# Mixer A's values as feature tiles turned by transposes, weight tiles fetched three ahead, bias tiles of several heads in one transfer

## The chip, the core and the metric

The kernel runs on one core of a Trainium2 chip. The metric is the device time of one execution in microseconds (us). The core's engines are TensorE (PE: matmuls, with PEld for its weight loads), VectorE (DVE), ScalarE (ACT), GpSimd (POOL) and SyncE (SP), which issues nearly all DMA transfers of this program from one queue, in order.

## The reference

One decoder layer for a prompt of 1024 tokens and 8 single-token samples, with shared weights:

```
h = RMSNorm(x)
qa, ka, va, za, qb, kb, vb, zb, qc, zc, ga, gb, gc = split(h @ w_in)
x + W_out( sum_i sigmoid(g_i) * P_i( mixer_i * silu(z_i) ) )
  mixer A: dilated causal attention, 8 heads x 64, patterns (window, stride) (128,1), (512,4), (2048,16),
           combined by their softmax denominators
  mixer B: sliding-window attention (128), 8 query heads, 2 kv heads x 64, with a learned sink per head
  mixer C: cross-attention, 4 heads x 128, into 256 memory tokens
  A and B add a relative-position bias (32 buckets); queries and keys are RMS-normed
```

Keys and values of A and B for prompt and samples, and of the memory, are outputs too. All is float32; the change concerns `va`, the 512 value columns of mixer A.

## The kernel before, in words

Every float32 product is made of three reduced-precision ones: each operand is split into a rounded part and a remainder (`hh` and `hl` of the normed input, `wh` and `wl` of a weight), and PE runs high x high, low x high, high x low. The prompt and the samples form one matrix of 1032 columns (tokens), kept as 8 feature tiles of 128 partitions and cut into three chunks of 344. A weight tile covers 128 output features (128 x 1024 numbers, 512 KB) and serves three units, one for each chunk; a unit is 24 matmuls (8 feature tiles x 3 products) into one PSUM bank `psD`, of which there are two. Then ACT evicts it.

A weight tile goes through three steps: a transfer into `wr` (`wfetch`, L289), a rounding into `wh` on ACT or POOL (`wlead`), and a subtraction into `wl` on DVE or POOL (`wrest`). Which tile is fetched when is set by `wpump`, `wnext` and `wget` (L307 to L338): `wahead(n, ...)` fetches all tiles below n; `wget` forces whatever is missing at the moment of use.

The order of all work is written by the program itself, as a recording. `main` yields after each half or whole unit; each yield is one `tick` (L241), which may put in a step of the attention pipeline (`rope`, with duos of two 128-blocks), a step of the sample work, deferred pieces (`when`), and a pump of weights. A class `Pace` keeps estimated engine times; `idle` (L236) says whether DVE and ACT lie less than 3 us behind PE in that estimate, and only then does the tick call `wpump`. Each engine then executes its own instructions strictly in the recorded order, waiting on semaphores; so does SP with its transfers.

Nearly all working tiles are slabs (128 x 1032 numbers), 47 buffers that are reused in turn (`SLABS`, L39): the first writer of a slab waits for the last readers of the tile that had it before. Small tiles have their own few buffers; the evicted values `c` have two.

After the memory's keys and values, the four query tiles of mixer C, and keys, values and queries of B comes `va_phase` (L744). Here the tokens lie on the partitions: for each half of the value columns (two weight tiles of `w_va`) and each block of 128 tokens (nine, the last with the 8 samples) 24 matmuls with 256 columns give psD; ACT evicts it into `c`; a transfer writes it to the output `o_va`; POOL rounds it and DVE subtracts, into a slab `vhl`; two transfers write that to the scratch arrays `vsc` (natural order) and `vsr` (stride order). `whold` holds back splits of further weights during the first five blocks. Then come queries and keys of A, the gates of z and g, the three branches and the output. Meanwhile the attention heads run, C first, then B, then A; A's heads read `vsc` and `vsr` with `v_load`, and fetch their bias (`bn`, `bias`) from the replicated table `rep` with `bias_tile`.

Of the kernel before, what the change touches and what calls it, by code (L numbers as in the profile page):

```python
# [30 lines left out]

AHEAD_FIRST, AHEAD = 3, 2
SPLIT_FIRST, SPLIT = 3, 2
# [137 lines left out]
class Kern:  # L171
# [153 lines left out]
    def wnext(self):  # L325

        i = self.wi
        if self.wr == i < self.wh and self.ok(self.wsp[i][0]):
            self.wahead(0, 0, i + 1)
        if not self.whold and self.wh == i < self.wd and self.ok(self.wraw[i]):  # L330
            self.wahead(0, i + 1, 0)

    def wpump(self):
        self.wahead(self.wi + self.wdepth, 0, 0)
        if self.wr < self.wh and (self.start and self.wr <= self.wi or self.ok(self.wsp[self.wr][0])):
            self.wahead(0, 0, self.wr + 1)
        if not self.whold and self.wh < min(self.wi + self.wsoon, self.wd) and self.ok(self.wraw[self.wh]):
            self.wahead(0, self.wh + 1, 0)  # L338
# [405 lines left out]
    def va_phase(self):  # L744
        nc, io = self.nc, self.io
        self.vsc, self.vsr = [self.dram([NP, 8, 2, 64], F32, "vhl") for _ in range(2)]

        def turn(half, v):
            p = self.psT()
            for t in range(2):  # L750
                nc.tensor.transpose(p[:, t * NS:(t + 1) * NS], v[:NS, t * P:(t + 1) * P], self.ident[:NS, :NS])
            nc.scalar.activation(self.vs_a[:, 2 * half:2 * half + 2], p[:, :2 * NS].rearrange("p (t b) -> p t b", t=2), AF.Copy)

        for half in range(2):
            cs = slice(half * 256, (half + 1) * 256)
            ws = [self.wget() for _ in range(2)]
            for tb in range(9):
                self.whold = tb < 5
                m = P if tb < 8 else NS
                d = self.ps("D", 2)  # L760
                s = slice(tb * P, tb * P + m)
                for j, (x, y, k) in enumerate(self.order(8)):
                    c = (k % 4) * 256
                    nc.tensor.matmul(d[:m, :256], self.h[k][y][:, s], ws[k // 4][x][:, c:c + 256], start=j == 0, stop=j == 23)
                v = self.small([P, CH], "c1", 2)[:, :256]
                nc.scalar.activation(v[:m], d[:m, :256], AF.Copy)
                nc.sync.dma_start(out=io["o_va"][tb * P:tb * P + m, cs], in_=v[:m])
                if tb < 8:
                    vhl = self.slab(F32R, "vhl")[:, :512]
                    v4 = vhl.rearrange("p (h x d) -> p h x d", h=4, x=2)  # L770
                    vv = v.rearrange("p (h d) -> p h d", h=4)
                    nc.gpsimd.tensor_scalar(v4[:, :, 0], vv, 1.0, 0.0, op0=ALU.mult, op1=ALU.add)
                    nc.vector.tensor_sub(v4[:, :, 1], vv, v4[:, :, 0].bitcast(F32))
                    nc.sync.dma_start(out=self.vsc[tb * P:(tb + 1) * P, 4 * half:4 * half + 4].rearrange("p h x d -> p (h x d)"),
                                      in_=vhl.bitcast(F32))
                    nc.sync.dma_start(out=ap(self.vsr, tb * P * 1024 + half * 512, [[1024, 4], [4096, 32], [1, 512]]), in_=vhl.bitcast(F32))
                else:
                    self.when([v], turn, half, v, banks=1)
                yield
            ws = None  # L780
        self.flags.add("va")

# [160 lines left out]
    def heads_b(self):  # L943
        K = self

        class Head:
# [8 lines left out]
            def prep(self):  # L955
# [10 lines left out]
                if self.h % 4 == 0:  # L966
                    K.bias_b, b = K.slab(F32, "bias"), K.slab(F32, "bn")
                    for j in range(4):
                        K.bias_tile(b[:, 256 * j:256 * j + 256], 2, self.h + j)
                    K.bias_turn(K.bias_b[:, :NP], b[:, :NP])  # L970
# [35 lines left out]
    def heads_a(self):  # L1006
        K = self

        class Head:
# [5 lines left out]
            def ready(self):  # L1015
                return ("qa", self.h // 2) in K.flags and "va" in K.flags

            def prep(self):
# [6 lines left out]
                if hh == 0:  # L1025
                    K.bias_a, b = K.slab(F32, "bias"), K.slab(F32, "bn")
                    for j in range(2):
                        K.bias_tile(b[:, 256 * j:256 * j + 256], 0, self.h + j)
                    for j in range(2):
                        K.bias_tile(K.bias_a[:, 256 * (2 + j):256 * (2 + j) + 256], 1, self.h + j)  # L1030
                    K.bias_turn(K.bias_a[:, :512], b[:, :512])
# [26 lines left out]
    def v_load(self, h, s):  # L1058
# [4 lines left out]
        if s == 0:  # L1063
            nc.sync.dma_start(out=vf.rearrange("p (b c) -> p b c", b=8), in_=ap(self.vsc, h * P, [[1024, P], [P * 1024, 8], [1, P]]))
        else:
            v4 = vf.rearrange("p (r b c) -> p r b c", r=4, b=2)
            for b in range(2):
                nc.sync.dma_start(out=v4[:, :, b], in_=ap(self.vsr, b * 512 * 1024 + h * P, [[4 * 1024, P], [1024, 4], [1, P]]))
        return v
# [155 lines left out]
    def samples(self):  # L1225
# [6 lines left out]
        for t in range(4):  # L1232
            while ("qb", t) not in self.flags or "vb" not in self.flags or "va" not in self.flags:
                yield ()
# [157 lines left out]
    def weights(self):  # L1392
# [16 lines left out]
        self.wi = self.wd = self.wh = self.wr = 0  # L1409
        self.wdepth, self.wsoon, self.whold = AHEAD_FIRST, SPLIT_FIRST, False  # L1410

    def main(self):
# [39 lines left out]
        def qk_a(t):  # L1452
            def done_a(i, x):
# [3 lines left out]
                else:  # L1457
# [426 lines left out]
def _layout(i):  # L1884
# [5 lines left out]
    a["w_in"] = _stat(w)  # L1890
    a["w_va"] = np.ascontiguousarray(w[:, 1024:1536].reshape(2, 4, P, 2, 256).transpose(3, 0, 2, 1, 4)).reshape(4, P, 1024)
    a["w_mk"] = _stat(g["w_mem_kv"][0][:, :512])
# [26 lines left out]

_OUTS = {"o_y": (8, P, NT), "o_ka": (4, P, NT), "o_va": (NT, 512), "o_kb": (P, NT), "o_vb": (P, NT), "o_mk": (P, 1024), "o_mv": (2, P, 512)}  # L1920

# [28 lines left out]
```

## Time and profile before

| | |
|---|---|
| runs | 1223.71, 1227.69, 1227.39 us (median 1227.39) |
| the profiled execution's own time | 1225.49 us |
| its span, first to last instruction | 1223.7 us, 19948 instructions |
| PE busy | 1151.8 us (94%), mean granted clock 0.971 |
| DVE / ACT / POOL busy | 654.5 / 472.2 / 502.5 us |
| DMA | 206.32 MB, 169 GB/s in the mean |

The span is what the profile sees of one execution; the execution's own time lies 1.8 us above it. In the rows below, `psD<-hh,wh` is a matmul that writes psD from those two operands; a note `[6.40 <-ACT wh L150]` says that the engine had been idle for 6.40 us and that an ACT instruction writing `wh` released it. All instructions are recorded through one helper, so every row names L150; rows are told apart by their tiles.

### The profile page before, as it was taken

The numbers are of one execution on the slowest core, as the hardware profiler recorded it, in microseconds if no ns is written. First come the engines' busy times: TensorE is split into PE (matmuls) and PEld (weight loads), VectorE is DVE, ScalarE is ACT, GpSimd is POOL, SyncE is SP. The second block draws the span as 40 slices with busy tenths as digits, with TensorE's granted clock in tenths as the row PEclk, the third lists the DMA queues.
The fourth block names the chain that finished last, engine by engine and source line by source line (L and its number), as shares of the span: only waits on it lengthen the run. The fifth ranks groups of instructions, "written<-read, shape, count | busy, mean of one in ns | idle before, by whom it ended". The sixth has DMA issues, their size and how long they took to land.

```text
span 1223.7 us, 19948 instructions
## 1 busy us (share of the span) xinstructions
PE 1151.8 (94%) x7540; PEld 1124.8 (92%) x7540; DVE 654.5 (53%) x1205; ACT 472.2 (39%) x1127; POOL 502.5 (41%) x411
## 2 busy tenths in 40 slices
PE   8889999986998999999997999999999989999898
PEld 7777999975998999999997999999999989999898
DVE  6664366443455676675645565554446646737311
ACT  5443355410455455565644455552112221212100
POOL 4354344121470433224442422261746536857300
PEclk9899999987999899999999999999999999999999
DMA  9302413476543445565464565455879689542331
GB/s 315 122 3 92 174 54 116 159 253 198 151 128 115 151 150 173 156 173 139 134 180 114 182 174 177 137 174 194 262 201 377 213 302 378 187 172 70 104 122 70
DMA packets 90181, 206.32 MB, mean 169 GB/s; under 512 B 14373, under 2 KB 40979, under 8 KB 90085
## 3 DMA queue, kind: packets, MB, share of 16 engines
q1 hardware_dynamic: 89940, 205.03, 52.4%
q8 instruction: 59, 0.97, 0.3%
q14 instruction: 38, 0.30, 0.1%
q10 hardware_dynamic: 144, 0.02, 0.0%
HBM read 154.98 MB, written 45.97 MB: 164 GB/s over the span
## 4 chain that ended last, share of the span: by engine, by line
PE 67%; DMA 13%; DVE 6%; POOL 5%; issue 4%; SPq 3%; ACT 2%; POOLq 0%; ACTq 0%; DVEq 0%
PE psD L150 38%; PE psO L150 12%; PE psSc L150 8%; PE psM L150 5%; PE psT L150 4%; SPq L150 3%; DMA wr<-w_in 3%; DMA o_va<-c 2%; DMA vhl<-vhl 2%; DVE wl L150 1%; DMA cv<-cmv 1%; DVE ml L150 1%; POOL c L150 1%; POOL sq L150 1%; POOL wl L150 1%
## 5 line engine op out<-in xcount | busy, mean ns | idle before, releaser
L150 PE MATMUL psD<-hh,wh 128*128 128x344 f32 x1088 | 357.9, 329 | 19.3 <-POOL wh L150 8.4
L150 PE MATMUL psD<-hh,wl 128*128 128x344 f32 x1088 | 352.9, 324 | 7.6 <-POOL wl L150 4.1
L150 PE MATMUL psD<-hl,wh 128*128 128x344 f32 x1088 | 353.0, 324 | 3.3 <-DVE hl L150 1.8
L150 PEld LDWEIGHTS psD<-hh,wh 128*128 128x128 f32 x1088 | 208.1, 191 | 23.2 <-POOL wh L150 8.7
L150 PEld LDWEIGHTS psD<-hh,wl 128*128 128x128 f32 x1088 | 208.2, 191 | 9.6 <-DVE wl L150 5.0
L150 PEld LDWEIGHTS psD<-hl,wh 128*128 128x128 f32 x1088 | 208.6, 192 | 5.2 <-DVE hl L150 2.6
L150 POOL TENSOR_TENSOR wl<-wr,wh 128x1024 fp32r<-128x1024 f32 (+1 forms) x41 | 93.1, 2272 | 56.2 <-ACT wh L150 54.5
L150 DVE TENSOR_TENSOR wl<-wr,wh 128x1024 fp32r<-128x1024 f32 (+1 forms) x58 | 74.6, 1292 | 57.6 <-ACT wh L150 29.1
L150 ACT ACTIVATE p<-psT 128x512 fp32r<-128x512 f32 (+2 forms) x112 | 61.9, 552 | 101.9 <-PE psT L150 98.3
L150 ACT ACTIVATE wh<-wr 128x1024 fp32r<-128x1024 f32 (+1 forms) x61 | 54.5, 901 | 109.5 <-DMA wr<-w_out 38.2
L150 POOL TENSOR_SCALAR wh<-wr 128x1024 fp32r<-128x1024 f32 (+1 forms) x38 | 40.2, 1058 | 135.9 <-DMA wr<-w_in 84.9
L150 POOL TENSOR_TENSOR c<-raw 128x344 f32<-128x344 f32 x51 | 45.0, 882 | 107.4 <-ACT raw L150 96.0
L150 POOL TENSOR_TENSOR cv<-cv,pb 128x1024 f32<-128x1024 f32 x24 | 59.6, 2493 | 69.5 <-DMA pb<-d 49.0
L150 DVE CUSTOM_DVE_ANT_0 L<-psSc,bias 128x256 f32<-128x256 f32 (+1 forms) x128 | 43.6, 378 | 61.3 <-PE psSc L150 60.5
L150 DVE TENSOR_TENSOR p<-psT,p 128x512 fp32r<-128x512 f32 (+2 forms) x112 | 70.7, 631 | 10.2 <-ACT p L150 9.0
L150 PE MATMUL psT<-ident,L 128*128 128x128 f32 x400 | 73.3, 275 | 0.0
L150 POOL TENSOR_TENSOR sg<-sg,sg 128x344 f32<-128x344 f32 x48 | 55.3, 1161 | 35.7 <-DVE sg L150 28.9
L150 POOL TENSOR_TENSOR ck<-ck,qbc 128x1024 f32<-128x1024 f32 x24 | 65.9, 2761 | 7.2 <-DMA qbc<-d 7.1
L150 ACT ACTIVATE L<-L,sta 128x256 f32<-128x256 f32 (+1 forms) x128 | 59.4, 467 | 19.7 <-DVE sta L150 19.6
L150 ACT ACTIVATE c<-psD 128x344 f32<-128x344 f32 (+2 forms) x54 | 23.3, 431 | 110.2 <-DMA o_va<-c 60.3
L150 PE MATMUL psD<-wh,hh 128*128 128x256 f32 (+1 forms) x144 | 45.1, 313 | 13.9 <-ACT c L150 13.8
L150 ACT ACTIVATE sq<-psD 128x344 fp32r<-128x344 f32 x51 | 23.2, 456 | 84.4 <-PE psD L150 73.9
(289 smaller groups left out, 2812.1 us busy)
## 6 DMA issues: line engine op xcount, KB each, us to landing
wr<-w_in SPq DMA_DIRECT2D x54, 512.0 KB
g<-sg SPq DMA_DIRECT2D x24, 516.0 KB
sg<-g SPq DMA_DIRECT2D x24, 516.0 KB
vhl<-vhl SPq DMA_DIRECT2D x32, 256.0 KB
pb<-d SPq DMA_DIRECT2D x32, 256.0 KB
rb<-d SPq DMA_DIRECT2D x26, 258.0 KB
qbc<-d SPq DMA_DIRECT2D x12, 512.0 KB
z<-sz SPq DMA_DIRECT2D x12, 512.0 KB
```

What stands on the lines that cost most here:

```text
L150: r = f(*a, **k)
```

## The change

Three things change. `va_phase` makes the values as feature tiles: four weight tiles of `w_in`, each with three units of 344 columns, evicted by ACT into one slab `va`, which one transfer writes to `o_va` (whose layout the host turns). For each tile two deferred `turn`s transpose four 128 x 128 blocks into a PSUM bank psT; from there ACT writes the rounded part and DVE the remainder of each of two heads into slabs `vhl`; after the second turn one transfer writes a head's slab to `vsc` and four write it to `vsr`, both now laid out head by head. The samples' values are copied from the slab by POOL. The flag is set per tile.

Weights: `AHEAD` goes from 2 to 3, each tick fetches up to that depth whether or not `idle` holds, and `whold` is gone.

Bias: `bias_tiles` fetches n heads with each of its four transfers, where `bias_tile` fetched one.

```diff
-AHEAD_FIRST, AHEAD = 3, 2
+AHEAD_FIRST, AHEAD = 3, 3
     def tick(self):
         self.tick_no += 1
         if not self.start:
+            self.wahead(self.wi + self.wdepth, 0, 0)
             self.wnext()
...
-        if not self.whold and self.wh == i < self.wd and self.ok(self.wraw[i]):
+        if self.wh == i < self.wd and self.ok(self.wraw[i]):
...
-    def bias_tile(self, dst, s, h):
+    def bias_tiles(self, dst, s, h, n):
         for g in range(4):
-            self.nc.sync.dma_start(out=dst[32 * g:32 * g + 32], in_=ap(self.rep[s], h * 32 * 384 + 127 - (32 * g if s == 1 else g),
-                                                                       [[383 if s == 1 else 380, 32], [1, 256]]))
+            self.nc.sync.dma_start(out=dst[32 * g:32 * g + 32].rearrange("p (h k) -> p h k", h=n),
+                                   in_=ap(self.rep[s], h * 32 * 384 + 127 - (32 * g if s == 1 else g), [[383 if s == 1 else 380, 32], [32 * 384, n], [1, 256]]))
...
     def va_phase(self):
         nc, io = self.nc, self.io
-        self.vsc, self.vsr = [self.dram([NP, 8, 2, 64], F32, "vhl") for _ in range(2)]
+        self.vsc = self.dram([8, P, NP], nm="vhl")
+        self.vsr = self.dram([8, NP, P], nm="vhl")
...
+        def turn(t, v, g, hs):
+            if not hs:
+                hs = [self.slab(F32R, "vhl") for _ in range(2)]
             p = self.psT()
+            for j in range(4):
+                nc.tensor.transpose(p[:, j * P:(j + 1) * P], v[:, (4 * g + j) * P:(4 * g + j + 1) * P], self.ident)
+            for hh in range(2):
+                x = hs[hh][:, g * 512:(g + 1) * 512].rearrange("p (b x d) -> p b x d", b=4, x=2)
+                pv = p.rearrange("p (b k d) -> p b k d", b=4, k=2)[:, :, hh]
+                nc.scalar.activation(x[:, :, 0], pv, AF.Copy)
+                nc.vector.tensor_sub(x[:, :, 1], pv, x[:, :, 0].bitcast(F32))
+            if g == 0:
+                self.when([], turn, t, v, 1, hs, banks=1)
+                return
+            for hh in range(2):
+                h, x = 2 * t + hh, hs[hh][:, :NP].bitcast(F32)
+                nc.sync.dma_start(out=self.vsc[h], in_=x)
+                for r in range(4):
+                    nc.sync.dma_start(out=ap(self.vsr, (h * NP + r) * P, [[4 * P, 32], [P * P, 8], [1, P]]),
+                                      in_=x[32 * r:32 * r + 32].rearrange("p (b c) -> p b c", b=8))
+            self.flags.add(("va", t))
-        for half in range(2):
...
+        for t in range(4):
+            w = self.wget()
+            v = self.slab(F32, "va")
+            for c in range(3):
                 d = self.ps("D", 2)
+                yield from self.fm(d, w, self.h, 8, c * CH, (c + 1) * CH)
+                nc.scalar.activation(v[:, c * CH:(c + 1) * CH], d[:, :CH], AF.Copy)
                 yield
+            nc.sync.dma_start(out=io["o_va"][t], in_=v)
+            nc.gpsimd.tensor_copy(self.vs_a[:, t], v[:, NP:NT])
+            self.when([v], turn, t, v, 0, None, banks=1)
...
-            nc.sync.dma_start(out=vf.rearrange("p (b c) -> p b c", b=8), in_=ap(self.vsc, h * P, [[1024, P], [P * 1024, 8], [1, P]]))
+            nc.sync.dma_start(out=vf, in_=self.vsc[h])
...
-        jobs.append(([(io["w_va"][j], 1024) for j in range(4)], None, lambda: self.va_phase()))
+        jobs.append(([wi(8 + j) for j in range(4)], None, lambda: self.va_phase()))
```

What stands where, at three places. The last number of a name counts upwards through the recording of all engines; the one before it counts named tiles, so a lower number was recorded earlier. First, the queue of SP around the fetch of the 29th weight tile in the order of use, `wr_688` before and `wr_623` now; `sz` to z are gates written out, `kh` and `kl` the split keys of a head, `rb` the rows of a norm, `ck` a cache tile of the samples. Before:

```order
L150 DMA kh_675_3828<-kh_675_3828 64x1024
L150 DMA kl_676_3829<-kl_676_3829 64x1024
L150 DMA qbc_684_3886<-d_665_3763 128x1024
L150 DMA rb_686_3889<-d_667_3769 64x1032 x2
L150 DMA wr_688_3907<-w_in 128x1024
L150 DMA wr_689_3909<-w_in 128x1024
L150 DMA z_46_113<-sz_663_3749 128x1024
```

and now:

```order
L150 DMA rb_602_3316<-d_595_3273 64x1032 x2
L150 DMA wr_605_3333<-w_in 128x1024
L150 DMA wr_623_3467<-w_in 128x1024
L150 DMA ck_629_3496<-cmk 128x1024
L150 DMA rb_642_3565<-d_595_3273 64x1032 x2
L150 DMA kh_644_3585<-kh_644_3585 64x1024
L150 DMA kl_645_3586<-kl_645_3586 64x1024
L150 DMA z_45_112<-sz_621_3453 128x1024
L150 DMA wr_656_3662<-w_in 128x1024
```

Before, `wr_688` is followed by its rounding into `wh_690` and its first matmul into `psD_693`. Now the 29th tile is `wr_623`, right behind the 28th and ahead of a head's keys; its first matmul writes `psD_677`.

Second, ACT's queue, with the semaphores that each row waits for (a DMAHW one is raised by a finished transfer). Before, in the values' phase, where `c1` is the small tile `c`:

```order
L150 ACTIVATE c1_482_2501<-psD_481_2476 128x256 [waits DMAHW6_49,DVE_49,PE_49]
L150 ACTIVATE wh_484_2509<-wr_450_2288 128x1024 [waits DMAHW4_49]
L150 ACTIVATE c1_487_2538<-psD_486_2513 128x256 [waits DMAHW4_49,DVE_49,PE_49]
L150 ACTIVATE c1_493_2578<-psD_492_2553 128x256 [waits DMAHW2_49,DVE_49,PE_49]
L150 ACTIVATE c1_496_2612<-psD_495_2587 8x256 [waits DMAHW5_49,DVE_49,PE_49]
```

and now, from the last value unit into the first unit of the job behind it:

```order
L150 ACTIVATE va_496_2645<-psD_512_2754 128x344 [waits PE_49]
L150 ACTIVATE vhl_529_2841<-psT_531_2843 128x4x64 [waits PE_49]
L150 ACTIVATE vhl_530_2842<-psT_531_2843 128x4x64 [waits DVE_49]
L150 ACTIVATE sq_532_2864<-psD_526_2824 128x344 [waits DMAHW5_49,DMAHW1_49,DMAHW6_49,DMAHW0_49,DMAHW7_49,PE_49,Activation_49]
L150 ACTIVATE raw_525_2823<-psD_526_2824 128x344 [waits DMAHW2_49]
L150 ACTIVATE vhl_529_2841<-psT_535_2871 128x4x64 [waits PE_49]
L150 ACTIVATE vhl_530_2842<-psT_535_2871 128x4x64 [waits DVE_49]
L150 ACTIVATE sq_537_2915<-psD_536_2890 128x344 [waits DMAHW3_49,PE_49,Pool_49]
L150 ACTIVATE raw_525_2823<-psD_536_2890 128x344
L150 ACTIVATE sq_540_2946<-psD_539_2921 128x344 [waits DMAHW5_49,DMAHW4_49,DMAHW6_49,DMAHW0_49,DMAHW7_49,PE_49,Activation_49]
```

Each eviction of values waited for a transfer, and now those of `va` wait for PE alone; the evictions behind them (`sq` is the square, `raw` the copy of a unit of keys or queries) wait for transfers.

Third, SP's queue where a pair of A's heads begins. Before:

```order
L150 DMA kh_1208_6947<-kh_1208_6947 64x1024
L150 DMA kl_1209_6948<-kl_1209_6948 64x1024
L150 DMA v_1210_6953<-vhl_437_2215 128x8x128
L150 DMA bn_1212_6956<-rep_206_908 32x256 x8
L150 DMA bias_1211_6955<-rep_207_909 32x256 x8
L150 DMA ck_1221_7049<-cbk 128x1024
L150 DMA d_1231_7123<-st_1222_7051 4x344 x3
L150 DMA wr_1232_7127<-w_in 128x1024
```

and now, at an earlier pair:

```order
L150 DMA kh_859_4857<-kh_859_4857 64x1024
L150 DMA kl_860_4858<-kl_860_4858 64x1024
L150 DMA v_861_4863<-vhl_415_2116 128x1024
L150 DMA bn_863_4866<-rep_207_910 32x2x256 x4
L150 DMA bias_862_4865<-rep_208_911 32x2x256 x4
L150 DMA wt_869_4912<-d_856_4839 64x1024 x2
L150 DMA z_44_111<-sz_841_4770 128x1024
L150 DMA wr_880_4987<-w_in 128x1024
```

Sixteen issues of one head's 32 KB are now eight of two heads' 64 KB, and `v` is read in whole rows.

More of the change, by code (lines that the diff above doesn't have):

```diff
@@ L336, in wpump @@
             self.wahead(0, 0, self.wr + 1)
-        if not self.whold and self.wh < min(self.wi + self.wsoon, self.wd) and self.ok(self.wraw[self.wh]):
+        if self.wh < min(self.wi + self.wsoon, self.wd) and self.ok(self.wraw[self.wh]):
             self.wahead(0, self.wh + 1, 0)
@@ L745, in va_phase @@
         nc, io = self.nc, self.io
-        self.vsc, self.vsr = [self.dram([NP, 8, 2, 64], F32, "vhl") for _ in range(2)]
-        def turn(half, v):
-            p = self.psT()
-            for t in range(2):
-                nc.tensor.transpose(p[:, t * NS:(t + 1) * NS], v[:NS, t * P:(t + 1) * P], self.ident[:NS, :NS])
-            nc.scalar.activation(self.vs_a[:, 2 * half:2 * half + 2], p[:, :2 * NS].rearrange("p (t b) -> p t b", t=2), AF.Copy)
-        for half in range(2):
[L755 to L759, printed above, removed]
-                d = self.ps("D", 2)
[L761 to L778, printed above, removed]
@@ L779, in va_phase @@
+        for t in range(4):
+            w = self.wget()
+            v = self.slab(F32, "va")
+            for c in range(3):
+                d = self.ps("D", 2)
+                yield from self.fm(d, w, self.h, 8, c * CH, (c + 1) * CH)
+                nc.scalar.activation(v[:, c * CH:(c + 1) * CH], d[:, :CH], AF.Copy)
                 yield
-            ws = None
-        self.flags.add("va")
+            nc.sync.dma_start(out=io["o_va"][t], in_=v)
+            nc.gpsimd.tensor_copy(self.vs_a[:, t], v[:, NP:NT])
+            self.when([v], turn, t, v, 0, None, banks=1)
@@ L967, in prep @@
                     K.bias_b, b = K.slab(F32, "bias"), K.slab(F32, "bn")
-                    for j in range(4):
-                        K.bias_tile(b[:, 256 * j:256 * j + 256], 2, self.h + j)
+                    K.bias_tiles(b[:, :NP], 2, self.h, 4)
                     K.bias_turn(K.bias_b[:, :NP], b[:, :NP])
@@ L1015, in ready @@
             def ready(self):
-                return ("qa", self.h // 2) in K.flags and "va" in K.flags
+                return ("qa", self.h // 2) in K.flags and ("va", self.h // 2) in K.flags
             def prep(self):
@@ L1026, in prep @@
                     K.bias_a, b = K.slab(F32, "bias"), K.slab(F32, "bn")
[L1027 to L1030, printed above, removed]
+                    K.bias_tiles(b[:, :512], 0, self.h, 2)
+                    K.bias_tiles(K.bias_a[:, 512:1024], 1, self.h, 2)
                     K.bias_turn(K.bias_a[:, :512], b[:, :512])
@@ L1067, in v_load @@
             for b in range(2):
-                nc.sync.dma_start(out=v4[:, :, b], in_=ap(self.vsr, b * 512 * 1024 + h * P, [[4 * 1024, P], [1024, 4], [1, P]]))
+                nc.sync.dma_start(out=v4[:, :, b], in_=ap(self.vsr, (h * NP + b * 512) * P, [[4 * P, P], [P, 4], [1, P]]))
         return v
@@ L1232, in samples @@
         for t in range(4):
-            while ("qb", t) not in self.flags or "vb" not in self.flags or "va" not in self.flags:
+            while ("qb", t) not in self.flags or "vb" not in self.flags or ("va", 3) not in self.flags:
                 yield ()
@@ L1409, in weights @@
         self.wi = self.wd = self.wh = self.wr = 0
-        self.wdepth, self.wsoon, self.whold = AHEAD_FIRST, SPLIT_FIRST, False
+        self.wdepth, self.wsoon = AHEAD_FIRST, SPLIT_FIRST
     def main(self):
@@ L1890, in _layout @@
     a["w_in"] = _stat(w)
-    a["w_va"] = np.ascontiguousarray(w[:, 1024:1536].reshape(2, 4, P, 2, 256).transpose(3, 0, 2, 1, 4)).reshape(4, P, 1024)
     a["w_mk"] = _stat(g["w_mem_kv"][0][:, :512])
@@ L1917, in _layout @@
     return a
-_OUTS = {"o_y": (8, P, NT), "o_ka": (4, P, NT), "o_va": (NT, 512), "o_kb": (P, NT), "o_vb": (P, NT), "o_mk": (P, 1024), "o_mv": (2, P, 512)}
+_OUTS = {"o_y": (8, P, NT), "o_ka": (4, P, NT), "o_va": (4, P, NT), "o_kb": (P, NT), "o_vb": (P, NT), "o_mk": (P, 1024), "o_mv": (2, P, 512)}
 def kernel(**inputs):
@@ L1940 @@
     ka = r["o_ka"].reshape(512, NT).T[rows].reshape(NT, 8, 64)
-    va = r["o_va"][rows].reshape(NT, 8, 64)
+    va = r["o_va"].reshape(512, NT).T[rows].reshape(NT, 8, 64)
     kb = r["o_kb"].T[rows].reshape(NT, 2, 64)
```

## The prediction

> **What bounds the kernel now.** I read the page's first part, then the waits of TensorE (PE), then windows laid around each wait.
>
> ```profile
> PE 1151.8 (94%) x7540; PEld 1124.8 (92%) x7540; DVE 654.5 (53%) x1205; ACT 472.2 (39%) x1127; POOL 502.5 (41%) x411
> ```
>
> PE is the bound: no other engine passes 53%. So time goes only where PE has less to do, stands idle or runs slowly. Its waits from 100 us on (the first 100 us are mostly untouched):
>
> ```profile
> PE psD L150 <- ACT c L150: 15.8, 7, 3.7
> PE psD L150 <- POOL wh L150: 8.4, 1, 8.4
> PE psD L150 <- POOL wl L150: 6.6, 3, 2.5
> PE psD L150 <- ACT wh L150: 6.4, 1, 6.4
> PE psD L150 <- DVE ml L150: 3.7, 3, 1.9
> PE psO L150 <- ACT wh L150: 2.9, 1, 2.9
> ```
>
> Two causes hold nearly all of it: `c`, the small tile into which the values of mixer A are evicted, and `wh`/`wl`, the two parts of a weight tile. Windows around them (columns: length, then busy us and count of PE, PEld, DVE, ACT, POOL, then the granted clock, DMA share, GB/s):
>
> ```profile
> 117.00:130.50 13.50, 13.50 (x87) 13.50 (x87) 5.90 (x4) 3.55 (x7) 2.92 (x4) 1.00 0.40 145
> 217.00:310.00 93.00, 73.14 (x500) 69.15 (x500) 34.95 (x40) 16.37 (x41) 20.19 (x26) 0.85 0.61 200
> 392.00:408.00 16.00, 9.22 (x46) 8.43 (x45) 3.42 (x8) 3.68 (x8) 8.51 (x5) 0.68 0.61 204
> 408.00:515.00 107.00, 107.00 (x756) 106.30 (x755) 76.76 (x177) 58.15 (x157) 31.60 (x25) 1.00 0.50 153
> 515.00:530.00 15.00, 13.16 (x85) 12.79 (x84) 9.30 (x27) 8.65 (x25) 5.87 (x4) 0.89 0.55 179
> 665.00:690.00 25.00, 16.32 (x102) 15.55 (x101) 9.44 (x20) 8.79 (x23) 7.27 (x9) 0.80 0.69 198
> 760.00:775.00 15.00, 12.78 (x80) 12.41 (x79) 5.94 (x20) 6.66 (x18) 11.10 (x6) 0.89 0.45 144
> 992.00:1010.00 18.00, 13.84 (x77) 13.27 (x76) 10.00 (x14) 5.50 (x7) 7.16 (x6) 0.91 0.98 309
> ```
>
> Between the events PE is full at clock 1.00 (408 to 515: 756 instructions, 0.1415 us each). In the values' phase it stands idle for 93.00 - 73.14 = 19.9 us and the clock falls to 0.85; in the five weight windows it is idle for 6.8 + 1.8 + 8.7 + 2.2 + 4.2 = 23.7 us. An idle stretch also halves the clock behind it: after the wait at 399 the starts lie 0.29 us apart, not 0.158.
>
> ```profile
> 399.47 0.65 PE L150 MATMUL psD<-hh,wh 128*128 128x344 f32 x1 [6.40 <-ACT wh L150]
> 401.24 0.49 PE L150 MATMUL psD<-hh,wh 128*128 128x344 f32 x1
> 401.53 0.49 PE L150 MATMUL psD<-hl,wh 128*128 128x344 f32 x1
> ```
>
> The whole loss of a window is its length less its work at full clock. The five weight windows hold 89 us and 390 instructions, at about 0.147 us 57 us: **32 us lost**. The phase's work comes next.
>
> **The values' phase.** What PE does there, as merged pieces of the chain, and what holds it (an ACT row, and a transfer of the chain):
>
> ```profile
> 226.44 2.86 PE psD L150 x24
> 430.42 3.79 PE psD L150 x24
> 310.09 0.87 PE psT L150 x8
> 306.17 0.38 PE L150 MATMUL psT<-ident,c 8*128 8x8 f32 x2 [1.57 <-ACT c L150]
> ACT c L150 <- DMA o_va<-c: 60.3, 14, 7.5
> 286.30 0.38 ACT L150 ACTIVATE c<-psD 128x256 f32<-128x256 f32 x1 [7.50 <-DMA o_va<-c]
> 287.51 8.81 DMA o_va<-c
> ```
>
> Work: 18 units of 24 matmuls at 2.86 are 51.5 us; the other 68 of the window's 500 instructions at the same 0.12 are 8.2. So 93 - 60 = **33 us lost**, 19.9 idle and 13 slow. Cause: two `c` tiles, each free only when its transfer to o_va has landed, 8.81 us after issue; ACT waits 60.3 us in 14 times, and behind it PE, which has two psD banks.
>
> New work: 12 units at 3.79 = 45.5, and 32 transposes at 0.87/8 = 0.11, 3.5 us; the four tiny transposes removed (a pair took 0.38, at half clock) are about 0.4. Sum 49.0 against 51.9: **-2.9**. The Trainium skill speaks against this term: "TensorE: Matmul & The Clock Gate", Part 4, PE-mode transpose, gives about 275 ns for one 128x128 transpose in a kernel, and says that transposing doesn't count as PE activity. As an estimate from that page, 32 would cost 8.8 us and the term would be +2.4. The trace's records are that long too, but they overlap: 0.11 from start to start.
>
> Evictions now go into a slab, as the one value tile of mixer B already does at 117 to 130 us, where PE is busy 13.50 of 13.50: the nearest row for the new phase. Their halves come like these:
>
> ```profile
> L150 ACT ACTIVATE vb<-psT x4: 367/381/384, 311.8 to 314.7; 128x256 fp32r<-128x256 f32 x4
> L150 DVE TENSOR_TENSOR vb<-psT,vb x4: 411/420/425, 313.0 to 315.1; 128x256 fp32r<-128x256 f32 x4
> L150 POOL COPY vsb<-vb x1: 189/189/189, 130.0 to 130.0; 128x8 f32<-128x8 f32 x1
> ```
>
> Sixteen of each are 6.1 us on ACT and 6.7 on DVE. ACT has 16.37 us of work in the 93, DVE 34.95: both hide it; without that cover the evictions behind them would wait, at most these 13 us. POOL loses its sixteen roundings and gains four copies of the eight sample columns, 0.2 us each.
>
> What can remain of the 33: at best nothing; at worst the idle time comes back through slabs. The 47 slabs turn round, and the order shows ACT's next `sq` and `raw` waiting for DMA queues, because their slabs held `vhl` and `va` tiles whose transfers must have read them. Behind such an ACT row wait the psD evictions and then PE. Between writing out `vhl_500` and its successor `sq_540` I count some 20 us of PE work, twice the 8.81 of a transfer; it can fail only if SP holds them back by 10. I take **4 us left**, so **-29** (bounds: -33 and -10, where all 19.9 idle and some clock comes back).
>
> **Weights three ahead.** What is late (timeline of the DMA queue of SP, of PE, and the startup):
>
> ```profile
> 390.62 1.07 SPq L150 DMA_DIRECT2D wr<-w_in  x2
> 657.10 5.46 SPq L150 DMA_DIRECT2D bn<-rep  x8
> 662.61 3.67 SPq L150 DMA_DIRECT2D bias<-rep  x8
> 667.89 0.83 SPq L150 DMA_DIRECT2D wr<-w_in  x2
> 674.21 0.65 PE L150 MATMUL psD<-hh,wh 128*128 128x344 f32 x1 [8.36 <-POOL wh L150]
> 63.75 0.43 PE L150 MATMUL psD<-hh,wh 128*128 128x344 f32 x1 [1.00 <-ACT wh L150]
> 65.72 0.43 PE L150 MATMUL psD<-hh,wl 128*128 128x344 f32 x1 [1.39 <-DVE wl L150]
> ```
>
> Both large stalls start with a fetch issued 6 to 9 us before PE goes on. In the order it was recorded directly ahead of the rounding and the first matmul (wr_688, wh_690, psD_693; likewise wr_1232): no PE work lay between. By the code, the planner's pump is skipped while it holds ACT or DVE for busy. Counting recorded matmuls at 3.79/24 from each fetch to its first use, the five windows belong to leads of 0, 0, 9.5, 11.6 and 13.3 us (6.5 and 13.5 got by); of the leads above 14 only one had a wait over 0.4, the 2.5 on `wl` at 221, split late. In the change the smallest lead from the values on is 15.1 (one half-size w_brc tile), next 18.9, and 23 or more up to the gates. A slab that isn't free delays a fetch at most to where PE stands when it is recorded, which these leads already assume, plus the lag of DVE, ACT or POOL.
>
> What remains: three places where the split is recorded right at its use, with the data there: wh_558/wl_563 ahead of psD_565, wl_668, and wh_1772/wl_1775. A split costs 1.0 to 2.5 us (the waits on `wl` above are 2.5 at most); with clock I put 2 on each and take **6 left**: **-26** (bounds: -32, and -16 if SP's own waits eat half the leads). In the startup the fourth query tile of mixer C is now fetched ahead of the x loads: of 1.00 + 1.39 I take **-1.5** (bounds -2.4 and +2, if the x parts of the last chunk, one transfer later, become late).
>
> **Bias in one transfer.** 96 issues become 40. The trace has no such form; the sixteen at 657 take 9.13 us of SP, so a pair's eight cost 4.6 if it goes by instructions, 9.1 if by bytes. It is hidden either way: the next weight stands ahead of them in the queue now. 0. The same for `vhl`: 40 issues instead of 32, o_va 4 instead of 18.
>
> **New waits.** More tiles are alive, so more writes wait for a slab. Bounds: none, or 8.81 for a write that meets a transfer just issued; I take **+3**.
>
> Sum: 1225.49 (the profiled execution, 1223.7 of span and 1.8 around it) - 2.9 - 29 - 26 - 1.5 + 3 = 1169.1. The median of the runs shown is 1.9 above that execution: **1171**.
>
> **Rivals.**
>
> *The leads don't reach the chip*: SP works in order and waits for ACT or DVE in front of a fetch, so half the weight loss stays. For: the 9 us that SP spent on bias in front of the fetch at 667.89. Against: the fetches now stand before such blocks. -26 becomes -10, and some 6 us of the same delay reach the values' phase: 1193.
>
> *The phase stays bound by its transfers*: the same bytes go out (share 0.61), now through slabs; ACT waits for slabs instead of `c`. For: the DMA waits on `sq` in the order. Against: 20 us between, and ten more slabs than two `c` tiles. -29 becomes -5: 1195.
>
> *Transposes that don't overlap*: each group of four stands alone behind an eviction, and a lone one lasts its record.
>
> ```profile
> L150 PE MATMUL psT<-ident,L x400: 270/272/421, 150.6 to 827.5; 128*128 128x128 f32 x134
> ```
>
> That is 32 x 0.272 = 8.7 instead of 3.5: 1176. Against it, eight of them took 0.87 in the chain. (This is what the Trainium skill's "TensorE: Matmul & The Clock Gate", Part 4, PE-mode transpose, would make of it.)
>
> *Slower*: the same at full price. Twelve slabs (eight `vhl`, four `va`) are written out in the phase; if each next ACT write waits one whole landing, 8.81 us, with PE behind, that is 106 against a gain of 59 before new waits: 1227.4 - 59 + 106 = 1274. It decides from the seventh full landing on (62 us). The fourteen waits on `c` averaged 4.3, with two tiles, which speaks against.
>
> *It does not do what it says*: fetches are recorded earlier but wait for slabs until as late as before, and the values' gain is spent on transposes and evictions: no difference, 1227.
>
> **Chances.** Forecast 0.68 (own range 1157 to 1186), transposes 0.03, leads 0.09, transfers 0.12 (faster in all four), slower 0.04, no effect 0.04. The range 1153 to 1198 takes in the best bounds (1225.5 - 2.9 - 33 - 32 - 2.4 + 1.9 = 1157, and a few us of small waits more) and the first two rivals. 0.3% is 3.7 us, about what these runs can tell: faster 0.92, same 0.04, slower 0.04.
>
> **What would show it.** Right: no PE wait on `c` (the line ACT c <- DMA o_va<-c gone); PE over 95% busy at clock 1.00 from the first value tile to the last; no single wait on `wh` above 3 us; 32 psT<-ident,va at 0.11 us in the chain; SP's bias rows down to 40. Wrong: ACT `sq`, `raw` or `vhl` waiting for vhl or o_va transfers with PE idle behind them; a PE wait on `wh` released by a late `wr`; or new PE waits on `p` or `yh`.

## The result and the profile after

The changed kernel takes 1164.1 us (1162.82 to 1166.08), the kernel before beside it 1225.7: a ratio of 0.9499, interval 0.9474 to 0.9524. The forecast was 1171, range 1153 to 1198. The profiled execution fell from 1225.49 to 1162.82, by 62.7.

The engines in the changed kernel (first part of its page):

```profile
PE 1125.8 (97%) x7424; PEld 1104.7 (95%) x7424; DVE 645.7 (56%) x1201; ACT 475.1 (41%) x1136; POOL 503.2 (43%) x402
```

PE's waits in it (total, times, longest), the rows of the weights and three others:

```profile
PE psD L150 <- DVE wl L150: 5.6, 3, 2.4
PE psD L150 <- DVE ml L150: 3.7, 3, 1.9
...
PE psT L150 <- DVE aw L150: 1.7, 1, 1.7
PE psD L150 <- DVE sz L150: 1.7, 1, 1.7
...
PE psD L150 <- ACT wh L150: 1.0, 1, 1.0
```

`c` is gone, and of the waits on `wh` one of 1.0 us is left. Windows of the kernel before, then of the changed one (length, busy us and count of PE, PEld, DVE, ACT, POOL, granted clock, DMA share, GB/s):

```profile
210.00:310.00 100.00, 80.14 (x553) 76.11 (x552) 38.36 (x45) 20.35 (x51) 22.85 (x28) 0.86 0.60 197
310.00:1130.00 820.00, 793.60 (x5289) 784.51 (x5288) 475.43 (x971) 345.60 (x854) 373.94 (x286) 0.98 0.59 184
```

```profile
210.00:285.00 75.00, 75.00 (x514) 74.62 (x513) 32.62 (x55) 31.34 (x76) 14.60 (x12) 1.00 0.74 228
285.00:301.00 16.00, 12.09 (x67) 11.18 (x66) 6.25 (x12) 6.45 (x16) 15.53 (x17) 0.89 1.03 338
301.00:1070.00 769.00, 761.39 (x5145) 754.98 (x5144) 467.06 (x948) 334.65 (x830) 353.54 (x272) 1.00 0.60 191
```

The whole values' phase runs without a gap at clock 1.00. Right behind it is the largest new stall, 3.9 us idle; from there to 1070 PE is idle for 7.6 us, where before it was 26.4 (820.00 - 793.60).

Counted as in the prediction (loss = length of a stretch less its matmuls at the full-clock price, 0.1575 us for 344 columns, 0.119 for 256), the two profiled executions differ like this:

| stretch | before | after | difference | predicted |
|---|---|---|---|---|
| work at full clock, whole kernel | 1086.3 | 1082.4 | -3.9 | -2.9 |
| loss up to the values (210 / 200 us) | 41.4 | 36.1 | -5.3 | -1.5 |
| loss in the values and just behind (to 310) | 32.8 | 9.4 | -23.4 | -29 + 3 |
| loss from 310 on | 60.0 | 29.8 | -30.2 | -26 |

They sum to -62.8. How a loss is divided depends on where the stretches are cut and on the prices taken for the other shapes, so a single difference is good to about 2 us.

### The profile page after: what moved, and what is told of

It reads as the page before. It is cut to its first block, busy times and chain, and to the rows that moved or that the text cites. A ratio compares the mean times of both kernels' runs of the same rounds, so it can differ in the third digit from the quotient of the medians.

```text
span 1161.0 us, 19631 instructions
## 1 busy us (share of the span) xinstructions
PE 1125.8 (97%) x7424; PEld 1104.7 (95%) x7424; DVE 645.7 (56%) x1201; ACT 475.1 (41%) x1136; POOL 503.2 (43%) x402
## 4 chain that ended last, share of the span: by engine, by line
PE 78%; DVE 6%; DMA 5%; POOL 4%; issue 3%; ACT 2%; SPq 1%; POOLq 0%; ACTq 0%; DVEq 0%
PE psD L150 46%; PE psO L150 14%; PE psSc L150 9%; PE psM L150 5%; PE psT L150 5%; DMA wr<-w_in 1%; DVE ml L150 1%; SPq L150 1%; DVE wl L150 1%; POOL sq L150 1%; DMA vhl<-vhl 1%; POOL c L150 1%; DMA bn<-rep 1%; DMA wr<-w_mk 1%; POOL wl L150 1%
## 5 line engine op out<-in xcount | busy, mean ns | idle before, releaser
L150 PE MATMUL psD<-hh,wh 128*128 128x344 f32 x1184 | 386.0, 326 | 3.9 <-DVE sz L150 1.7
L150 PE MATMUL psD<-hh,wl 128*128 128x344 f32 x1184 | 380.7, 322 | 4.7 <-DVE wl L150 4.7
L150 PE MATMUL psD<-hl,wh 128*128 128x344 f32 x1184 | 381.1, 322 | 2.3 <-POOL hl L150 1.4
L150 PEld LDWEIGHTS psD<-hh,wh 128*128 128x128 f32 x1184 | 224.1, 189 | 6.8 <-DVE sz L150 1.9
L150 PEld LDWEIGHTS psD<-hh,wl 128*128 128x128 f32 x1184 | 224.2, 189 | 5.3 <-DVE wl L150 5.3
L150 PEld LDWEIGHTS psD<-hl,wh 128*128 128x128 f32 x1184 | 224.4, 190 | 4.0 <-POOL hl L150 2.7
L150 POOL TENSOR_TENSOR wl<-wr,wh 128x1024 fp32r<-128x1024 f32 (+1 forms) x45 | 106.3, 2362 | 50.6 <-ACT wh L150 48.4
L150 DVE TENSOR_TENSOR p<-psT,p 128x512 fp32r<-128x512 f32 (+2 forms) x112 | 70.7, 631 | 14.1 <-ACT p L150 13.4
L150 POOL TENSOR_TENSOR sq<-c,sq 128x344 fp32r<-128x344 f32 x51 | 52.0, 1020 | 4.0
L150 PEld LDWEIGHTS psT<-ident,L 128*128 128x128 f32 x400 | 48.7, 140 | 0.2
```

Source lines behind the costliest of these rows:

```text
L150: r = f(*a, **k)
```

## The experiments

Each is given with its ratio to the kernel before, measured on the same chip, and the 95% interval. The kernel before ran in 1213 to 1230 us there, so half a per cent is little. The forecasts start from the 1225.7 us above, or from the changed kernel's 1164.1; the medians of the kernel before were 1219.2 to 1221.7 here, so a forecast is judged by its ratio.

**What held the values' phase.** The prediction named the two `c` tiles. One line makes `c` a slab:

```diff
-                v = self.small([P, CH], "c1", 2)[:, :256]
+                v = self.slab(F32, "c")[:, :256]
```

> The kernel before with one line changed: in the old values' phase, c is one of the 47 slabs and no longer one of two small tiles. Work, order of the values and their 128 KB transfers stay. If the two tiles are the cause of the phase's 33 us, most of it goes without any transposes: -25, 1201 (1196 to 1207), and the ACT wait of c for DMA o_va (60.3 us) is gone. Rival (the phase is bound by its transfers, DMA share 0.61, or by POOL's roundings): the wait moves to slabs or to vhl, and the time is 1216 or more.

Measured: 1216.8 against 1219.2, ratio 0.9974 (0.9935 to 1.0013): no difference. ACT's waits in its phase (217 to 335 us):

```profile
ACT c L150 <- PE psD L150: 22.7, 11, 3.7
ACT c L150 <- DMA vhl<-vhl: 20.8, 3, 12.0
ACT wh L150 <- DMA wr<-w_in: 13.1, 2, 7.1
...
ACT c L150 <- DMA o_va<-c: 4.9, 2, 3.6
```

The wait only moved: from o_va, 60.3 us, to slabs that wait for `vhl` transfers, up to 12.0 us at a time. So the rival stands, the phase is bound by its transfers; but its DMA share is just 0.60. The next experiments bear on why.

The new phase alone, without the weights and the bias:

```diff
-        jobs.append(([(io["w_va"][j], 1024) for j in range(4)], None, lambda: self.va_phase()))
+        jobs.append(([wi(8 + j) for j in range(4)], None, lambda: self.va_phase()))
```

(with `va_phase`, `v_load`, the flags and the output's layout from the change)

> The kernel before with the new values' phase alone (feature tiles, transposes, whole-head writes and the loads that go with them; a tile's split may start during the phase). Weights stay two ahead and are fetched as before, bias tiles stay in single transfers. In the order two of its fetches after the phase still have no PE work between them and their use (wr_620, wr_707), as two had before. By the terms of the prediction the phase brings -2.9 - 29 + 3 = -29: 1225.7 - 29 = 1197 (1190 to 1203), with PE waits of 6 to 8 us on wh left at two places and none on c. Rival (the phase gains only because weights come early, or stays bound by its transfers): less than half of that, 1211 or more.

Measured: 1201.2, ratio 0.9851 (0.9780 to 0.9922), some 18 us, not the 29 expected. The phase itself gains (PE is busy for 113.0 of the 118 us from 217 to 335, before for 97.5). Of the two expected waits on `wh` one has 6.86 us (at 399) and the other 1.87, and a larger one, which was not expected, stands near the end. Timelines of SP and of PE:

```profile
954.48 8.19 SPq L150 DMA_DIRECT2D pb<-d  x6
962.72 1.54 SPq L150 DMA_DIRECT2D wr<-w_brc  x3
...
969.91 0.65 PE L150 MATMUL psO<-yh,wh 128*128 128x344 f32 x1 [13.39 <-ACT wh L150]
```

A weight fetch stands behind six transfers that hold SP for 8.19 us, for 6.2 of which SP itself waits for earlier transfers to land (the DMA share is 1.01 from 954 to 963): the weights' own problem, in a place where the kernel before lost 2.9 us.

Then the writes themselves. In the changed kernel each head is written once in natural order and in four pieces for the stride order. This kernel writes it once, in an order from which both can be read (the natural form with the same address pattern as the write, the stride form in four pieces):

```diff
-                nc.sync.dma_start(out=self.vsc[h], in_=x)
-                for r in range(4):
-                    nc.sync.dma_start(out=ap(self.vsr, ...), in_=x[32 * r:32 * r + 32]...)
+                nc.sync.dma_start(out=ap(self.vsc, h * P * NP, [[NP, 4], [4 * NP, 32], [1, NP]]), in_=x)
```

> The changed kernel with each head's values written out once (in an order from which both forms can be read) instead of once plus four row pieces: 8 transfers of vhl in place of 40, 4 MB less; the row form is read in four pieces instead of two (32 in place of 16). Theory: the stall at 294 to 301 (0.96 and 2.35 us idle, some 5 us with the slow clock) is a wl whose slab was vhl and whose five transfers stood 9.41 us in SP; one transfer frees it early: -4, 1160 (1156 to 1163). Rival (the slab waits for the 512 KB transfer itself, 7.65 us): 1164, no difference. Against it: sixteen more issues at 0.54 us each in the main phases, hidden on SP, or +3 where a late fetch stands behind them.

Measured: 1199.4, ratio 0.9835 (0.9802 to 0.9868): both expectations are far off. With 32 transfers fewer in the phase it loses some 34 us against the changed kernel. In its chain of waits and in one of its windows:

```profile
240.72 15.29 DMA ck<-cmk
...
264.21 15.22 DMA o_va<-va
```

```profile
271.00:272.00 1.00, 1.00 (x10) 1.00 (x9) 0.00 (x0) 1.00 (x2) 0.00 (x0) 1.00 0.26 102
272.00:273.00 1.00, 1.00 (x9) 1.00 (x8) 0.67 (x1) 0.56 (x2) 0.00 (x0) 1.00 0.25 102
273.00:274.00 1.00, 1.00 (x8) 1.00 (x8) 0.88 (x2) 0.03 (x1) 0.00 (x0) 1.00 0.25 102
...
276.00:277.00 1.00, 1.00 (x8) 1.00 (x8) 0.48 (x2) 0.85 (x2) 0.00 (x0) 1.00 0.26 107
```

After two of the new writes are issued at 270, the DMA share stands at a quarter for six microseconds, 102 to 107 GB/s: as much as four engines of sixteen. The outermost step of that write has four entries (`[NP, 4]`). Transfers issued around such writes land after 15 us. Not all of the 34 us lies here: from 420 to 800 us, where the natural form is read with four outermost entries too, PE is idle for 11.2 us against 4.7 in the changed kernel, and the engines have another order there. Now the same bytes in natural order, with 128 partitions outermost; the row form is read in eight pieces with 32 outermost. Here the planner is charged as in the changed kernel, so that PE, ACT, DVE and POOL have exactly its order:

```diff
+                nc.sync.dma_start(out=self.vsc[h], in_=x)
...
+                for g in range(4):
+                    self.nc.nc.sync.dma_start(out=v4[32 * g:32 * g + 32, :, b],
+                        in_=ap(self.vsc, h * P * NP + (4 * b + g) * P, [[NP, 32], [32 * NP, 4], [1, P]]))
```

> The changed kernel with each head's values written once in the natural form and the row form read from it in eight pieces: 8 transfers of vhl in place of 40, 64 loads of 64 KB in place of 16 of 256 KB, the planner charged as in the changed kernel, so that the order of PE, ACT, DVE and POOL is exactly that of the changed kernel. Theory A (the stall at 294 to 301 is the slab of wl, held by vhl's five transfers; and the 35 us that the first form with one write lost came from writes whose outermost address step has four entries, so that few DMA engines share 512 KB): the stall shrinks by 2 us or more, 1161 (1157 to 1164). Theory B (those 35 us came from the pieces in which the row form is read): it loses again, 1175 or more, with waits on v in the main phases of mixer A. Theory C (the one 512 KB write holds the slab as long): no difference.

Measured: 1160.7, ratio 0.9494 (0.9465 to 0.9523). Theory A holds: no plateau, no loss (theory B falls), and the stall behind the phase shrinks. One of its windows, with a full DMA:

```profile
271.00:277.00 6.00, 6.00 (x42) 5.96 (x41) 3.35 (x6) 2.24 (x6) 2.56 (x2) 1.00 1.03 285
```

It differs from the kernel above in the write, in both reads and in the order of the engines, so the pair tells that the four-entry patterns go with the plateau, and not what each costs. The wait on `wl` behind the phase fell from 2.35 to 1.29 us, that on `wh` stayed at 0.96. Whether it beats the changed kernel (0.9552, 0.9518 to 0.9587, in one comparison, 0.9499 in another) is not settled by these times: the two did not run on the same chip.

The kernel before has the same plateau:

```profile
292.00:294.00 2.00, 2.00 (x17) 2.00 (x16) 1.15 (x1) 0.33 (x1) 0.88 (x1) 0.84 0.25 81
306.00:308.00 2.00, 1.83 (x7) 1.80 (x8) 0.00 (x0) 0.30 (x2) 0.00 (x0) 0.50 0.30 102
```

Its write to `vsr` was `[[1024, 4], [4096, 32], [1, 512]]`: four outermost, 16 times 256 KB. Counting the packets in flight over the trace, by their starts and durations, exactly four fly for 11 of its phase's 93 us, and five to twelve for 32; in the changed kernel's 75 us it is 0.4 and 4.7. That these writes caused the 33 us of the kernel before is thus inferred from the plateau and from the pair above; the old phase with its writes cut into pieces was not run.

The Trainium skill has the rule: "DMA: Bandwidth & Descriptors", section "Why a DMA increments its semaphore by 16 and not by 1", says that a transfer uses the largest number of engines up to 16 that divides the slowest dimension of both of its access patterns. For 4 and 128 that is 4; for 32 and 32, or 128 and 128, it is 16. The traces agree, with shares of 0.25 and 1.03.

**What took the weight waits.** A lead is the PE work recorded between a weight's fetch and its first use. The fetch at each tick alone, two tiles ahead, in the kernel before:

```diff
         if not self.start:
+            self.wahead(self.wi + self.wdepth, 0, 0)
             self.wnext()
```

> The kernel before with the fetch at every planner step alone, still two tiles ahead (three, with the old values' phase holding two split tiles at once, need more slabs than there are). In the order the leads of 0, 0, 6.5 and 11.6 us are gone; 13.5 and 9.5 at the end stay. By the prediction's term the four windows between 392 and 775 lose their stalls but for some 6 us and the window at 992 keeps its own: -26 + 6 = -20, 1206 (1200 to 1211), and the values' phase still waits on c. Rival (leads don't reach the chip, SP holds them back): the weights bring 10, 1216. Rival (three ahead is what counts): no more than 5, 1221.

Measured: 1206.2, ratio 0.9872 (0.9793 to 0.9950), some 16 us by the ratio. The microseconds are the forecast's, but the kernel before was quicker there too: the interval holds the theory (1206 of 1225.7 is 0.984) and also the first rival (1216, 0.992), and leaves out the second. Its trace decides. Its PE waits from 200 us on:

```profile
PE psD L150 <- ACT c L150: 17.5, 9, 4.3
...
PE psD L150 <- ACT wh L150: 2.2, 1, 2.2
```

The waits of 6.4 and 8.4 on `wh` are gone, so the leads do reach the chip; `c` stays, and the last one (2.2, at 967) is where its leads are still 13.5 and 9.5. Now the changed kernel without that line, with three tiles ahead:

```diff
         if not self.start:
-            self.wahead(self.wi + self.wdepth, 0, 0)
             self.wnext()
```

> The changed kernel without the fetch at every planner step: three tiles ahead, but recorded only by the pump that is skipped while ACT or DVE counts as busy, as before. In its order two fetches stand directly ahead of their use (wr_679, wr_712) and two more have 12.4 and 12.9 us of PE work. Theory (a lead of nothing is a stall of 6 to 9 us and as much again at a slow clock, some 10 each): two such waits on wh, near 345 and 362 us, +20 to the changed kernel: 1184 (1177 to 1191). Rival (the values' phase and the single bias transfer make the fetch early enough by themselves): 1165.

Measured: 1180.7, ratio 0.9662 (0.9635 to 0.9690): the theory (1184 of 1225.7 is 0.966). The changed kernel did not run on that chip; by its two ratios elsewhere, 0.9552 and 0.9499, this is 13 to 20 us above it. Its PE timeline has the two waits at the two fetches without a lead, at 365 and 393 us where 345 and 362 were expected:

```profile
364.75 0.66 PE L150 MATMUL psD<-hh,wh 128*128 128x344 f32 x1 [9.05 <-POOL wh L150]
...
392.93 0.66 PE L150 MATMUL psD<-hh,wh 128*128 128x344 f32 x1 [6.34 <-ACT wh L150]
```

And the changed kernel with the fetch at each tick, but two tiles:

```diff
-AHEAD_FIRST, AHEAD = 3, 3
+AHEAD_FIRST, AHEAD = 3, 2
```

> The changed kernel with two tiles ahead instead of three; the fetch at every planner step stays. In its order the leads are 18.9 us and more, but for the first w_brc tiles with 13.2, 9.5 and 15.1. Theory (the fetch at every step removes the stalls, the third tile adds little): at most the window at the first w_brc tiles comes back, some 3 to 6 us over the changed kernel's 1164.1: 1167 (1163 to 1171). Rival (the third tile is what counts, as the wait of 13.39 us on wh at 969 suggests, which the new values' phase with the old fetching showed): 1177 or more.

Measured: 1166.1, ratio 0.9557 (0.9525 to 0.9589), against 0.9552 with three. The third tile brings nothing that the times can show. The traces show both sides: the waits at the first w_brc tile (a weight of the branches) are back (2.05 and 1.82 us), so are two of the startup (1.00 and 1.39 us), and what stood behind the values' phase is smaller in its order, 0.68 us on `wl` in place of 2.35.

**The bias in one transfer.** Alone, in the kernel before:

```diff
-                    for j in range(4):
-                        K.bias_tile(b[:, 256 * j:256 * j + 256], 2, self.h + j)
+                    K.bias_tiles(b[:, :NP], 2, self.h, 4)
```

(and likewise two heads at a time for mixer A)

> The kernel before with bias tiles of several heads in one transfer alone. By the prediction nothing: 1225.7 (1222 to 1229). Rival: the block of sixteen issues stands in front of the late fetch at 667.89 (bn and bias took 5.46 + 3.67 us of SP); if eight issues take half, that fetch comes 4.6 us sooner and PE's 8.36 us wait on wh shrinks by as much, and as much again at the other blocks: 1221 or less.

Measured: 1202.9, ratio 0.9850 (0.9757 to 0.9942), some 18 us. The prediction's zero is wrong here; the rival has the direction, but the gain is well beyond its 4.6 us. The planner's account charges each transfer, 450 ns of a common queue among other things; with 56 transfers fewer it records PE's work in another order, and the fetch that had no lead (wr_1232) has none such in its place: the tiles there have leads of 19.9 and 25.9 us. So the same edit with the planner charged for the single transfers, which keeps every engine's order as before:

```diff
+            self.nc.nc.sync.dma_start(out=dst[32 * g:32 * g + 32].rearrange("p (h k) -> p h k", h=n), in_=...)
+        for j in range(n):
+            for g in range(4):
+                self.pace.note("sync", "dma_start", ...)
```

> The kernel before with bias tiles of several heads in one transfer, while the planner is charged for the single transfers it would have issued, so that the order of every engine but SP's bias rows is that of the kernel before. Theory (the 16 us that the merged transfers alone brought come from another order, in which the fetch with no lead at 667 and two with short leads are gone, and not from the transfers): no difference to the kernel before (within 4 us), and the waits of 8.4 us on wh at 674 and 6.4 at 399 stay. Rival (SP's sixteen issues of 9.13 us held the late fetch back): the wait at 674 shrinks by 4 us or more, and the time by as much or twice as much: 0.995 or less.

Measured: 1212.9, ratio 0.9926 (0.9904 to 0.9948): some 9 us come from the transfers themselves, more than the theory's 4. The time is the rival's, its wait only half: SP and PE at the late fetch, which before had 5.46 + 3.67 us of SP ahead of it and a wait of 8.36:

```profile
652.68 2.27 SPq L425 DMA_DIRECT2D bn<-rep  x4
655.00 3.90 SPq L425 DMA_DIRECT2D bias<-rep  x4
...
667.73 0.65 PE L150 MATMUL psD<-hh,wh 128*128 128x344 f32 x1 [6.29 <-POOL wh L150]
```

The wait shrinks by 2.1 us, and the wait of 2.22 us on `wl` at 763, behind the next bias block, is gone. Eight issues take 6.17 us, 1.6 of them a wait of SP for a `v` to land (4.4 to 4.7 at the other places); sixteen took 9.13. So SP's price for these goes by issues, and a late fetch behind them gains. From 420 to 800 us, the kernel before, this one, and the merged transfers with their own order:

```profile
420.00:800.00 380.00, 366.72 (x2541) 362.20 (x2539) 232.72 (x589) 206.69 (x559) 137.11 (x110) 0.98 0.54 158
```

```profile
420.00:800.00 380.00, 371.09 (x2578) 367.10 (x2577) 236.53 (x600) 210.20 (x568) 139.45 (x112) 0.98 0.55 163
```

```profile
420.00:800.00 380.00, 379.77 (x2671) 377.00 (x2670) 243.44 (x618) 215.15 (x584) 139.15 (x113) 1.00 0.56 170
```

In these single executions PE is idle for 13.3, 8.9 and 0.2 us: a third of the gain there is the transfers, the rest the order. The times alone don't divide it so, since the two intervals overlap. Last, the changed kernel with single transfers:

> The changed kernel with single bias transfers, 96 issues as before. The leads in its order are as good as in the changed kernel (15.1 and more). Theory (with the fetch at every step the merged transfers add nothing of their own): within 5 us of the changed kernel, 0.952 to 0.959 of the kernel before, the 5 being what another order may do. Rival (they bring the 16 us that they brought alone): 1180, 0.968.

Measured: 1169.8, ratio 0.9581 (0.9551 to 0.9611), against 0.9552 (0.9518 to 0.9587) on another chip: inside the theory's range, and no clear difference. With early fetches there is little left for the merged transfers to bring.

**The price of a transpose.** Each transpose of the values three times:

```diff
-            for j in range(4):
+            for j in (0, 1, 2, 3) * 3:
```

> The changed kernel with every transpose of the values done three times into the same bank: 64 more, nothing else added. Theory (they overlap, 0.11 us from start to start): +7.0, 1171 (1168 to 1175). Rival (each lasts its record of 0.272, or the 275 ns that the Trainium skill's page TensorE: Matmul & The Clock Gate, Part 4, PE-mode transpose, gives): +17.4, 1181, and the clock falls after them.

> The changed kernel itself, as the measure for the other three on the same chip: 0.950 of the kernel before.

Measured: 1162.5, ratio 0.9538 (0.9503 to 0.9574); the changed kernel beside it 1165.3, 0.9552 (0.9518 to 0.9587; 0.950 was expected). Its chain and window, where each group is now twelve:

```profile
232.60 1.31 PE psT L150 x12
```

```profile
210.00:285.00 75.00, 75.00 (x536) 74.61 (x535) 35.68 (x62) 32.70 (x79) 15.42 (x17) 1.00 0.71 222
```

1.31/12 = 0.109 us each, at clock 1.00: the forecast price, 7.0 us of work for 64, and not the rival's 0.272. Yet the time did not rise to the 1171 expected. The planner counts the transposes too, and its other order has none of the waits that the changed kernel beside it shows between 288 and 300 (1.45, 1.12, 0.96, 2.34 us). So an accident of order can be worth as much as 64 transposes.

## Why the prediction was right, and where it was wrong

**The bound and the place of the loss**: right. PE's idle time and the slow clock behind it were the gain, but for some 4 us of work; the two groups of windows gave -23 and -30 of -62.7. The signs that the prediction named came: no wait on `c`, PE busy for 75.00 of 75.00 us of the values at clock 1.00, no wait on `wh` above 1.0, four transposes in 0.44 us, 40 bias rows. The forecast sum of -56.4 was 6 us short, in the startup and the weights.

**Work of the values' phase**, -2.9: right by its price. The chain has 0.44 us for four transposes. Of the Trainium skill's two statements ("TensorE: Matmul & The Clock Gate", Part 4, PE-mode transpose) its 275 ns agree with a record, 272 ns, but not with what one costs in a row, 0.109 us; of the second, that transposing doesn't count as PE activity, nothing shows here, as the clock stayed at 1.00 with twelve in a row.

**Values' stalls**, -29 and +3 for new waits: the size held (-23.4 against a net -26), the cause did not. The step that failed is "Cause: two `c` tiles, each free only when its transfer to o_va has landed": with `c` in slabs nothing was gained. As far as the plateaus show, the transfers were late because the writes to `vsr` next to them ran on a quarter of the DMA engines; that is inferred, not shown. The change cut that write into four pieces with 32 outermost, for its layout; the prediction read this as "40 issues instead of 32" and missed it. That the size held with the wrong cause is partly luck: it was taken from the measured loss, and the change happened to remove another cause of the same loss. By the same inference the rival "the phase stays bound by its transfers" did not come true, though the DMA share rose from 0.61 to 0.74 and, behind the phase, 1.03.

**Where the new wait is**: right in place, wrong in kind. It was to be ACT behind a `vhl` slab; it is DVE's `wl` (named as wl_563 among the three late splits), whose slab was `vhl`. SP, PE and DVE of the changed kernel:

```profile
282.43 9.41 SPq L150 DMA_DIRECT2D vhl<-vhl  x10
...
294.28 0.42 PE L150 MATMUL psD<-hh,wh 128*128 128x344 f32 x1 [0.96 <-ACT wh L150]
...
297.21 0.46 PE L150 MATMUL psD<-hh,wl 128*128 128x344 f32 x1 [2.35 <-DVE wl L150]
...
295.51 1.64 DVE L150 TENSOR_TENSOR wl<-wr,wh 128x1024 fp32r<-128x1024 f32 x1 [0.55 <-DMA vhl<-vhl]
```

Ten writes hold SP for 9.41 us while the DMA is full, "SP holds them back by 10", the condition under which the prediction let it fail. Of the 2.35 us the slab is the smaller part: DVE stood for the transfer for 0.55 us, and with one write a head 1.29 us stay, which are the late split itself. The loss there is some 6 us, against 4 + 2 + 3 set aside. The other two late splits cost 0.6 us at most, which is most of why the stretch from 310 on brought -30 and not -26; the merged bias has its part in that stretch too.

**Weights three ahead**: the mechanism was right, the name was not. The unconditional fetch does it; behind the startup the count of three does not show in the time (0.9557 against 0.9552). The rival "the leads don't reach the chip" fell with the trace of the fetch alone, whose waits of 6.4 and 8.4 are gone; its time does not exclude it.

**Bias**, "hidden either way": wrong alone, where it stood in front of late fetches (some 9 us); inside the change, where "the next weight stands ahead of them in the queue now", no run shows a difference. Of the two prices for a merged block, "by instructions" was the right one: 4.4 to 4.7 us for eight issues.

**Startup**, -1.5: it measured -5.3, past its bound of -2.4. The two waits that were counted on, 1.00 and 1.39, went with the third tile ahead: they are in the trace of every kernel with two tiles ahead, and in none with three. More went than was counted, the 1.19 on `hl` at 99 among it; but that one is there, 1.20 at 97, when each head is written once in the changed kernel's order, and it is gone when the kernel before has merged bias transfers in its old order. So part of the -5.3 is chance.

The three parts alone (values, fetch, bias) gave -18, -16 and -18 us by their ratios, which are not terms to add: each of them emptied most of the same stretch, 420 to 800 us, and the values alone made a wait of 13.4 that the fetch removes.

## What to carry to other kernels

A DMA share that stands at a quarter while other transfers wait was here the mark of a transfer that uses few engines: look at the outermost count of its addresses before blaming buffers. A fetch recorded under a condition ("when the engines are not busy") came late here just where they were; record it always, and test depth apart from condition. Where a planner sets the order, price an edit with the order held still, since a new order alone moved this kernel by several microseconds either way.

## What the runs showed that was not expected

- Two 512 KB writes whose outermost step has 4 entries, in flight together, ran at 102 to 107 GB/s and a share of 0.25 to 0.26. A `ck` tile issued right behind another such pair took 15.29 us to land.
- SP's price of the bias transfers goes by issues, not by bytes: sixteen of one head took 9.13 us, eight of two heads 4.4 to 4.7, or 6.2 with a wait of SP in it.
- Under a full DMA (share 1.03) ten writes held SP for 9.41 us, 0.94 each, where bias transfers took 0.57. The issues themselves are not dearer: for some 3.5 of the 9.41 us SP waited for earlier transfers to land, which leaves some 0.6 each. Its waits from 282 to 292:

```profile
SPq L150 <- DMA wr<-w_in: 1.4, 2, 0.8
SPq L150 <- DMA rb<-d: 1.2, 2, 0.7
SPq L150 <- DMA o_va<-va: 0.7, 1, 0.7
SPq L150 <- DMA vhl<-vhl: 0.2, 1, 0.2
```

- Sixty-four transposes more (7.0 us of PE) changed the time by less than can be measured, because the order changed with them.
